# A third pair of k-tiles by seven products in the gate and up projections of a hybrid decoder block

## The chip, the cores and the metric

One Trainium2 chip, and one core of it. The metric is the device time of one execution of the whole program in microseconds. The weights and the activations lie in HBM in float32.

## The reference

One decoder block over 256 tokens of width 2048: a mix of attention heads and mLSTM heads, then a feed-forward layer of width 5632, then a gated per-layer embedding. The change lies in the feed-forward layer:

```python
h2 = rms_norm(x, w_norm_ffn[i])
x = x + (jax.nn.silu(h2 @ w_ffn_gate[i]) * (h2 @ w_ffn_up[i])) @ w_ffn_down[i]
```

`w_ffn_gate` and `w_ffn_up` are 2048 x 5632, `w_ffn_down` is 5632 x 2048. The results are wanted in float32 accuracy.

## The kernel before

TensorE multiplies operands of a shortened float32 type, so each float32 operand is held as two halves: `h`, the value rounded to that type, and `l`, what is left. `halves` (L215) makes the two from a weight piece of 1024 elements per partition: ScalarE casts `wr` to `wh` (L220), and VectorE subtracts to get `wl` (L221). Each product of two float32 tiles is then three matmuls, high by high, high by low and low by high.

Gate and up run over 11 chunks of 512 columns (L769), numbered 1 to 11 here (the program's `c` is one less). A chunk needs the products of 16 k-tiles of 128 rows with two blocks of 128 tokens and two weights. The k-tiles are taken in eight pairs, 0 to 7, and each pair is one *unit*. A **plain unit** (L685) loads 512 KB of gate and 512 KB of up, makes halves of both, and issues 24 matmuls: two k-tiles, two token blocks, two weights, three matmuls each. Its results go to four banks of PSUM, P2, P3, P4 and P8.

Pairs 1 and 2 are **seven units** (L699). A pair of k-tiles, two token blocks and the two weights form a 2 x 2 by 2 x 2 product, which Strassen's scheme in Winograd's form does with seven block products where the plain way has eight. The four combinations of the activations, `fh` and `fl`, are made once for all chunks (`make_forms`, L657). The combinations of the weights are made anew in every chunk: four adds of 512 elements on VectorE (L702, L703, L705, L706) into two tiles `wt`, and then halves of the gate piece, of both `wt` tiles and of half the up piece. So a seven unit issues 21 matmuls and makes four `wh` and `wl` tiles, where a plain unit issues 24 and makes two. Its products P1, P6, P7 and P5 have banks of their own. After the last seven unit of a chunk these are drained (L748 to L755: a ScalarE copy and four VectorE adds), and at the end of the chunk VectorE folds the eight banks and forms silu(gate) times up (L757 to L766, with a sigmoid on ScalarE), then transposes it blockwise (L187). The transposed tile goes to HBM and back through GpSimd's queue (L191, L196), and is split in halves some units later (L129, L130).

All eight banks are in use; the two groups of four change roles from chunk to chunk (L718). The pool for weights (L34) has four buffers each of `wr`, `wh` and `wl`. A load waits in SyncE's queue until the buffer of two units before is free. The engines run in parallel, each strictly in its own order, and wait by semaphores. The order on each engine is set when the program is built, by a scheduler that places what it takes to be ready: neither the source's order nor a change in one line tells where an instruction stands.

Of the kernel before, what the change touches and what calls it, by code (L numbers as in the profile page):

```python
# [7 lines left out]
F32 = mybir.dt.float32  # L8
F32R = mybir.dt.float32r
BF16 = mybir.dt.bfloat16  # L10
# [9 lines left out]
def block_kernel(ctx, tc, x, p, w_norm_mix, w_in, fox_f_bias, q_norm_w, k_norm_w, conv_w, conv_b,  # L20
# [39 lines left out]
    rows_b = const.tile([82, P], F32, name="rows_b")  # L60

# [51 lines left out]
    def sumsq(dst, src):  # L113
        sq = small.tile([P, 512], BF16, name="sq")
        n = src.shape[-1]
        nc.scalar.activation(sq[:, 0:n], src, AF.Square, accum_out=dst)
# [151 lines left out]
    with tc.tile_pool(name="mixp", bufs=1) as mp:  # L268
# [40 lines left out]
        tasks = {}  # L309

# [334 lines left out]
    with tc.tile_pool(name="ffnp", bufs=1) as fp:  # L645
        acts_g = []

        def after_up(dst, gg):
            yield from split_by_blocks(dst, lambda b: gg[b])
# [3 lines left out]
        seven = (1, 2)  # L653
        first_order, later_order = (0, 3, 4, 1, 5, 2, 6, 7), (0, 3, 1, 4, 5, 2, 6, 7)
# [44 lines left out]
        def seven_unit(c, p):  # L699
            ra, rb = (load_piece(w, 2 * p, 2, c * 512, 512) for w in (w_gate, w_up))  # L700
            t12 = fp.tile([P, 2, 512], F32, name="wt", bufs=2)
            nc.vector.tensor_tensor(t12[:, 0], ra[:, 0], rb[:, 0], op=ALU.subtract)  # L702
            nc.vector.tensor_tensor(t12[:, 1], t12[:, 0], rb[:, 1], op=ALU.add)  # L703
            t34 = fp.tile([P, 2, 512], F32, name="wt", bufs=2)
            nc.vector.tensor_tensor(t34[:, 0], t12[:, 1], ra[:, 0], op=ALU.subtract)  # L705
            nc.vector.tensor_tensor(t34[:, 1], ra[:, 1], t12[:, 1], op=ALU.subtract)  # L706
            ah, al = halves(ra)
            h12, l12 = halves(t12)
            bh, bl = halves(rb[:, 1:2])
            h34, l34 = halves(t34)  # L710
            right = {"P1": (ah[:, 0], al[:, 0]), "P6": (h12[:, 1], l12[:, 1]), "P5": (h12[:, 0], l12[:, 0]),
                     "P2": (ah[:, 1], al[:, 1]), "P7": (h34[:, 0], l34[:, 0]), "P4": (h34[:, 1], l34[:, 1]),
# [3 lines left out]
        def gate_up(c):  # L716
# [4 lines left out]
            order = first_order if c == 0 else later_order  # L721
            left = {"P1": len(seven), "P6": len(seven), "P7": len(seven), "P5": len(seven), "P8": 16 - 2 * len(seven),
                    **{n: 16 - len(seven) for n in ("P2", "P3", "P4")}}
            bank, t1, qr, su = {}, None, None, None
            for p in order:
                advance(1)
                if p in seven:
# [8 lines left out]
                advance(1)  # L736
                for n, (lh, ll), (rh, rl) in unit:
# [7 lines left out]
                if su is None and left["P1"] == 0:  # L745
                    while held:
                        advance(1)
                    t1 = fp.tile([P, 512], F32, name="sg", bufs=2)  # L748
                    nc.scalar.copy(t1, bank["P1"])
                    qr = quads.tile([P, 2, 512], F32, name="quad")  # L750
# [112 lines left out]
```

## Time and profile before

| | |
|---|---|
| median of 3 runs | 1221.85 us (1220.7 to 1222.06) |
| the profiled execution | 1227.3 us |
| its span, first to last instruction | 1225.1 us |
| busy: TensorE, VectorE, ScalarE | 1211.5, 854.3, 622.8 us |
| granted TensorE clock, mean | 0.998 |
| gate and up, from the end of chunk 1 to the end of chunk 11 | 431.5 us |

A busy time is the time in which an engine had an instruction under way. TensorE's matmuls overlap: one takes 0.39 us from start to end, and the next starts after 0.23 us. So a group's mean duration is not what a matmul costs; the step from start to start is. The same holds, by less, for VectorE, whose instructions overlap by some 0.08 us. The time of a stage is read from the start of an instruction that occurs once per chunk.

### The profile page before, as it was taken

To read this page: it belongs to the slowest core of one execution; us is meant where nothing else is said; L and a number is where in the kernel's file an instruction comes from. 1 tells how busy PE (TensorE), PEld (TensorE's weight loads), DVE (VectorE), ACT (ScalarE), POOL (GpSimd) and SP (SyncE) were. 2 spreads that over 40 slices of the span, in tenths; PEclk is the share of its full clock that TensorE was granted. 3 is DMA by queue.
4 is the path that set the end of the run, shared out by engine and by line. 5 is a ranking of instruction groups with operands and counts; after the bars stand their busy time and mean duration, and the time that the engine had idled before them with its cause. 6 is when DMAs were issued, how large, how long until landed. Compare 5 with 4: busy or idle time off the path is not lost. (4 is left out here: it accounts for less than half of the span.)

```text
span 1225.1 us, 15485 instructions
## 1 busy us (share of the span) xinstructions
PE 1211.5 (99%) x5609; PEld 1003.9 (82%) x5609; DVE 854.3 (70%) x1188; ACT 622.8 (51%) x823; POOL 79.5 (6%) x149
## 2 busy tenths in 40 slices
PE   9999999999999999999999999999999999999998
PEld 6899978878888787888788888878888888888888
DVE  5766755565565898888879889888855554545754
ACT  6555556545555545555544555554544444446542
POOL 1111000000011000000000000000000000000000
PEclk9999999999999999999999999999999999999999
DMA  7677744575678667676676776667676666665762
GB/s 262 213 233 221 236 138 131 173 227 157 202 239 254 192 204 232 219 217 210 209 253 194 234 219 216 222 208 251 201 262 206 212 210 210 208 206 170 232 227 92
DMA packets 136384, 257.33 MB, mean 210 GB/s; under 512 B 10002, under 2 KB 29300, under 8 KB 136308
## 3 DMA queue, kind: packets, MB, share of 16 engines
q1 hardware_dynamic: 127156, 229.06, 59.2%
q0 software_dynamic: 8400, 26.22, 6.6%
q8 instruction: 44, 0.72, 0.2%
q10 hardware_dynamic: 752, 1.06, 0.2%
q14 instruction: 32, 0.26, 0.1%
HBM read 241.10 MB, written 15.20 MB: 209 GB/s over the span
## 5 line engine op out<-in xcount | busy, mean ns | idle before, releaser
L221 DVE TENSOR_TENSOR wl<-wr,wh 128x1024 fp32r<-128x1024 f32 (+2 forms) x445 | 508.6, 1154 | 289.4 <-ACT wh L220 288.5
L220 ACT CAST wh<-wr 128x1024 fp32r<-128x1024 f32 (+2 forms) x445 | 439.0, 997 | 449.2 <-PE acc L264 259.1
L262 PE MATMUL acc<-wh,act_h 128*128 128x512 f32 (+2 forms) x864 | 320.6, 371 | 0.1
L263 PE MATMUL acc<-wl,act_h 128*128 128x512 f32 (+2 forms) x864 | 318.0, 368 | 1.6 <-DVE wl L221 1.6
L264 PE MATMUL acc<-wh,act_l 128*128 128x512 f32 (+2 forms) x864 | 317.8, 368 | 0.0
L263 PEld LDWEIGHTS acc<-wl,act_h 128*128 128x128 f32 x864 | 163.0, 189 | 25.8 <-DVE wl L221 2.9
L262 PEld LDWEIGHTS acc<-wh,act_h 128*128 128x128 f32 x864 | 163.1, 189 | 24.6 <-ACT act_h L133 0.9
L264 PEld LDWEIGHTS acc<-wh,act_l 128*128 128x128 f32 x864 | 162.8, 188 | 24.5 <-DVE act_l L135 0.6
L191 POOL DMA_DIRECT2D swap<-tq x100 | 61.0, 616 | 882.1 <-DVE tq L187 882.1
L743 PE MATMUL acc<-wl,act_h 128*128 128x512 f32 x272 | 107.0, 393 | 0.1
L744 PE MATMUL acc<-wh,act_l 128*128 128x512 f32 x272 | 106.0, 390 | 0.0
L742 PE MATMUL acc<-wh,act_h 128*128 128x512 f32 x272 | 103.7, 390 | 0.0
L263 PE MATMUL acc<-wl,gh 128*128 128x512 f32 x224 | 88.3, 394 | 0.0
L262 PE MATMUL acc<-wh,gh 128*128 128x512 f32 x224 | 87.8, 392 | 0.0
L264 PE MATMUL acc<-wh,gl 128*128 128x512 f32 x224 | 86.9, 388 | 0.0
L220 ACT CAST wh<-wt 128x1024 fp32r<-128x1024 f32 x44 | 46.2, 1050 | 55.4 <-DVE wt L703 54.4
L742 PE MATMUL tr<-wh,act_h 128*128 128x512 f32 x178 | 69.5, 391 | 0.2 <-ACT wh L220 0.2
L743 PE MATMUL tr<-wl,act_h 128*128 128x512 f32 x178 | 69.7, 392 | 0.0
L744 PE MATMUL tr<-wh,act_l 128*128 128x512 f32 x178 | 69.3, 389 | 0.0
L743 PEld LDWEIGHTS acc<-wl,act_h 128*128 128x128 f32 x272 | 51.0, 188 | 13.7 <-DVE wl L221 3.3
L742 PEld LDWEIGHTS acc<-wh,act_h 128*128 128x128 f32 x272 | 51.1, 188 | 11.0
L744 PEld LDWEIGHTS acc<-wh,act_l 128*128 128x128 f32 x272 | 51.1, 188 | 10.4
(259 smaller groups left out, 1328.2 us busy)
## 6 DMA issues: line engine op xcount, KB each, us to landing
wr<-in_w_ffn_gate_dram SPq DMA_DIRECT2D x88, 512.0 KB, 3.5
wr<-in_w_ffn_up_dram SPq DMA_DIRECT2D x88, 512.0 KB, 4.5
wr<-in_w_ffn_down_dram SPq DMA_DIRECT2D x88, 512.0 KB, 4.6
wr<-in_w_in_dram SPq DMA_DIRECT2D x63, 512.0 KB, 4.7
wr<-in_w_in_dram SPq DMA_DIRECT2D x48, 344.0 KB, 3.7
wr<-in_w_out_dram SPq DMA_DIRECT2D x32, 512.0 KB, 4.3
wr<-in_w_ple_gate_dram SPq DMA_DIRECT2D x32, 512.0 KB, 4.6
swap<-tq POOLq DMA_DIRECT2D x100, 128.0 KB, 3.6
```

Source lines behind the costliest of these rows:

```text
L191: nc.gpsimd.dma_start(out=d[:, :, :, i, :].rearrange("j c b e -> c b j e"), in_=t[32 * i:32 * i + 32].rearrange("c b j k r -> c b j (k r)"))
L220: nc.scalar.copy(wh, wr)
L221: nc.vector.tensor_tensor(wl, wr, wh.bitcast(F32), op=ALU.subtract)
L262: nc.tensor.matmul(po[b][:, 0:n], ah[:, kk, s], wh[:, j, :], start=count == 1, stop=False)
L263: nc.tensor.matmul(po[b][:, 0:n], ah[:, kk, s], wl[:, j, :], start=False, stop=False)
L264: nc.tensor.matmul(po[b][:, 0:n], al[:, kk, s], wh[:, j, :], start=False, stop=count == total)
L742: nc.tensor.matmul(bank[n], lh, rh, start=first, stop=False)
L743: nc.tensor.matmul(bank[n], lh, rl, start=False, stop=False)
L744: nc.tensor.matmul(bank[n], ll, rh, start=False, stop=left[n] == 0)
```

## The change

From chunk 2 on, pair 4 is a seven unit too, and the order of the units becomes 0, 3, 1, 5, 2, 6, 4, 7. Chunk 1 keeps two seven units. The forms of pair 4 are made once, in chunk 2. Inside a seven unit the halves of the gate piece come first, then the first `wt` and its halves, then the second and its halves, and at the end those of the up piece; the products go P1, P2, P6, P5, P7, P4, P3. The draining of P1, P6, P7 and P5 stands one unit later in the source, behind the loads and halves of the unit that follows. The sigmoids write into the tile `quad` that the drained sums leave. To make room, `rows_b` moves to a pool that ends before gate and up, `sq` has one buffer in place of two, `t1` has a tile of its own, and at the end `acts_p` and the weights of the last norm use the two `wt` tiles (two loads of 1024 columns where there were four of 512). The way through HBM waits three units in place of two at each step.

```diff
-        seven = (1, 2)
-        first_order, later_order = (0, 3, 4, 1, 5, 2, 6, 7), (0, 3, 1, 4, 5, 2, 6, 7)
+        first_seven, seven = (1, 2), (1, 2, 4)
+        first_order, later_order = (0, 3, 4, 1, 5, 2, 6, 7), (0, 3, 1, 5, 2, 6, 4, 7)
...
             ra, rb = (load_piece(w, 2 * p, 2, c * 512, 512) for w in (w_gate, w_up))
+            ah, al = halves(ra)
             t12 = fp.tile([P, 2, 512], F32, name="wt", bufs=2)
             nc.vector.tensor_tensor(t12[:, 0], ra[:, 0], rb[:, 0], op=ALU.subtract)
             nc.vector.tensor_tensor(t12[:, 1], t12[:, 0], rb[:, 1], op=ALU.add)
+            h12, l12 = halves(t12)
             t34 = fp.tile([P, 2, 512], F32, name="wt", bufs=2)
             nc.vector.tensor_tensor(t34[:, 0], t12[:, 1], ra[:, 0], op=ALU.subtract)
             nc.vector.tensor_tensor(t34[:, 1], ra[:, 1], t12[:, 1], op=ALU.subtract)
-            ah, al = halves(ra)
-            h12, l12 = halves(t12)
+            h34, l34 = halves(t34)
             bh, bl = halves(rb[:, 1:2])
-            h34, l34 = halves(t34)
-            right = {"P1": (ah[:, 0], al[:, 0]), "P6": (h12[:, 1], l12[:, 1]), "P5": (h12[:, 0], l12[:, 0]),
-                     "P2": (ah[:, 1], al[:, 1]), "P7": (h34[:, 0], l34[:, 0]), "P4": (h34[:, 1], l34[:, 1]),
+            right = {"P1": (ah[:, 0], al[:, 0]), "P2": (ah[:, 1], al[:, 1]), "P6": (h12[:, 1], l12[:, 1]),
+                     "P5": (h12[:, 0], l12[:, 0]), "P7": (h34[:, 0], l34[:, 0]), "P4": (h34[:, 1], l34[:, 1]),
                      "P3": (bh[:, 0], bl[:, 0])}
...
-                if p in seven:
+                if p in by_seven:
...
+                if su is None and left["P1"] == 0:
+                    while held:
+                        advance(1)
+                    t1 = fp.tile([P, 512], F32, name="t1")
+                    nc.scalar.copy(t1, bank["P1"])
...
                 for n, (lh, ll), (rh, rl) in unit:
...
-                if su is None and left["P1"] == 0:
-                    while held:
-                        advance(1)
-                    t1 = fp.tile([P, 512], F32, name="sg", bufs=2)
-                    nc.scalar.copy(t1, bank["P1"])
...
-                sg = fp.tile([P, 512], F32, name="sg", bufs=2)
+                sg = qr[:, b]
...
-            if c == 0:
-                for kp in seven:
-                    Task(make_forms(kp), [made_by[id(acts_h[kp // 2][0])]])
+            for kp in (first_seven, [kp for kp in seven if kp not in first_seven], ())[min(c, 2)]:
+                Task(make_forms(kp), [made_by[id(acts_h[kp // 2][0])]])
```

The change moves instructions on every engine of this stage. In what follows `wl` and `wh` are halves of weights with their buffer numbers; line numbers of the changed file are up to two less in the first part and shift by a few in the second.

VectorE at the end of chunk 4, before. `wl_5213` is the up half of pair 0 of chunk 5, and `wl_5252` and `wl_5258` are the halves of its pair 3:

```order
L221 TENSOR_TENSOR wl_5213<-wr_5210,wh_5212 128x1024
L757 TENSOR_TENSOR gg0_5185<-acc0_4865,sg_5105 128x512
L759 TENSOR_TENSOR tq_5110<-acc1_4869,tq_5110 128x512
L758 TENSOR_TENSOR gg1_5186<-acc0_4873,quad_5107 128x512
L765 SCALAR_TENSOR_TENSOR gg0_5185<-gg0_5185,rstd_ffn_3032,sg_5191 128x512
L760 TENSOR_TENSOR tq_5110<-acc1_4877,tq_5110 128x512
L766 SCALAR_TENSOR_TENSOR gg0_5185<-tq_5110,rstd_ffn_3032,gg0_5185 128x512
L765 SCALAR_TENSOR_TENSOR gg1_5186<-gg1_5186,rstd_ffn_3032,sg_5195 128x512
L221 TENSOR_TENSOR wl_5252<-wr_5249,wh_5251 128x1024
L766 SCALAR_TENSOR_TENSOR gg1_5186<-tq_5110,rstd_ffn_3032,gg1_5186 128x512
L221 TENSOR_TENSOR wl_5258<-wr_5255,wh_5257 128x1024
L187 STREAM_TRANSPOSE tq_5201<-gg0_5185 128x512
```

and now, where `wl_5243` and `wl_5249` are the gate and the up half of pair 0 of chunk 5:

```order
L219 TENSOR_TENSOR wl_5243<-wr_5240,wh_5242 128x1024
L756 TENSOR_TENSOR gg0_5223<-acc0_4892,t1_5191 128x512
L758 TENSOR_TENSOR tq_5196<-acc1_4896,tq_5196 128x512
L757 TENSOR_TENSOR gg1_5224<-acc0_4900,quad_5193 128x512
L759 TENSOR_TENSOR tq_5196<-acc1_4904,tq_5196 128x512
L764 SCALAR_TENSOR_TENSOR gg0_5223<-gg0_5223,rstd_ffn_3032,quad_5193 128x512
L764 SCALAR_TENSOR_TENSOR gg1_5224<-gg1_5224,rstd_ffn_3032,quad_5193 128x512
L765 SCALAR_TENSOR_TENSOR gg0_5223<-tq_5196,rstd_ffn_3032,gg0_5223 128x512
L765 SCALAR_TENSOR_TENSOR gg1_5224<-tq_5196,rstd_ffn_3032,gg1_5224 128x512
L219 TENSOR_TENSOR wl_5249<-wr_5246,wh_5248 128x1024
L185 STREAM_TRANSPOSE tq_5237<-gg0_5223 128x512
```

The up half of chunk 5's first unit stood ahead of the fold of chunk 4 and now stands behind all of it, behind the instruction that waits for chunk 4's last product (L760, now L759). Chunks 2, 4, 6, 8 and 10 end like this; chunks 3, 5, 7 and 9 have that half inside the fold, behind its first instruction, and the transposes between the two halves of pair 3.

TensorE some 14 matmuls into chunk 5, now (`wh_5242` is of pair 0's gate, `wh_5287` of pair 3's, `wh_5327` of pair 1's gate):

```order
L752 MATMUL tr_5265<-wh_5242,act_h_3209 128x512
L753 MATMUL tr_5265<-wl_5243,act_h_3209 128x512
L754 MATMUL tr_5265<-wh_5242,act_l_3210 128x512
L752 MATMUL tr_5257<-wh_5287,act_h_3381 128x512
L752 MATMUL tr_5265<-wh_5287,act_h_3381 128x512
L752 MATMUL acc0_5349<-wh_5327,act_h_3209 128x512
L753 MATMUL sc_5261<-wl_5249,act_h_3209 128x512
L754 MATMUL sc_5261<-wh_5248,act_l_3210 128x512
L753 MATMUL sc_5269<-wl_5249,act_h_3209 128x512
L754 MATMUL sc_5269<-wh_5248,act_l_3210 128x512
```

Before, the first matmul with pair 0's low up half was the fifth of a chunk. Now (`wl_5249`) it is the 18th, behind matmuls of pairs 3 and 1 that need only high halves.

VectorE in chunk 5 from pair 5's gate half (`wl_5377`) to pair 2's, now (`wr_5414` and `wr_5416` are pair 2's gate and up loads, `wt_5422` its first sums, `wl_5426` their low half):

```order
L219 TENSOR_TENSOR wl_5377<-wr_5374,wh_5376 128x1024
L219 TENSOR_TENSOR wl_5383<-wr_5380,wh_5382 128x1024
L219 TENSOR_TENSOR wl_5419<-wr_5414,wh_5418 128x1024
L702 TENSOR_TENSOR wt_5422<-wr_5414,wr_5416 128x512
L128 TENSOR_TENSOR act_l_5236<-quad_5321,act_h_5235 128x512 x2
L703 TENSOR_TENSOR wt_5422<-wt_5422,wr_5416 128x512
L706 TENSOR_TENSOR wt_5429<-wt_5422,wr_5414 128x512
L707 TENSOR_TENSOR wt_5429<-wr_5414,wt_5422 128x512
L219 TENSOR_TENSOR wl_5426<-wt_5422,wh_5425 128x1024
```

Before, the halves that come back from HBM (L130, now L128) stood ahead of L702. They now stand between L702 and L703 of pair 2, which moved from the sixth to the fifth place of the chunk.

## Rows read from the trace of the kernel before

**Rows 1.** The page, busy time of each engine over the span.

```profile
PE 1211.5 (99%) x5609; PEld 1003.9 (82%) x5609; DVE 854.3 (70%) x1188; ACT 622.8 (51%) x823; POOL 79.5 (6%) x149
```

**Rows 2.** Windows view, gate and up: busy us (count) by engine, clock, DMA share.

```profile
447.00:877.00 430.00, 428.24 (x1856) 345.09 (x1855) 370.02 (x440) 225.30 (x250) 29.91 (x50) 1.00 0.69 219
```

**Rows 3.** View of line L757, once per chunk: first and last start.

```profile
L757 DVE TENSOR_TENSOR gg<-tr,sg x6: 681/684/692, 446.6 to 878.1; 128x512 f32<-128x512 f32 x6
```

**Rows 4.** Timeline of TensorE: a plain unit, a seven unit, a wait.

```profile
500.52 0.39 PE L742 MATMUL tr<-wh,act_h 128*128 128x512 f32 x1
...
502.33 0.39 PE L744 MATMUL acc<-wh,act_l 128*128 128x512 f32 x1
...
503.44 0.40 PE L744 MATMUL acc<-wh,fl 128*128 128x512 f32 x1
...
507.16 0.40 PE L742 MATMUL tr<-wh,act_h 128*128 128x512 f32 x1
...
606.11 0.50 PE L743 MATMUL acc<-wl,fh 128*128 128x512 f32 x1 [0.26 <-DVE wl L221]
606.45 0.39 PE L744 MATMUL acc<-wh,fl 128*128 128x512 f32 x1
```

**Rows 5.** Timeline of VectorE at the end of chunk 2: start, us.

```profile
492.11 0.68 DVE L760 TENSOR_TENSOR tq<-acc,tq 128x512 f32<-128x512 f32 x1
492.71 0.74 DVE L766 SCALAR_TENSOR_TENSOR gg<-tq,rstd_ffn,gg 128x512 f32<-128x512 f32 x1
493.37 0.74 DVE L765 SCALAR_TENSOR_TENSOR gg<-gg,rstd_ffn,sg 128x512 f32<-128x512 f32 x1
494.04 1.22 DVE L221 TENSOR_TENSOR wl<-wr,wh 128x1024 fp32r<-128x1024 f32 x1
495.17 0.74 DVE L766 SCALAR_TENSOR_TENSOR gg<-tq,rstd_ffn,gg 128x512 f32<-128x512 f32 x1
...
496.97 1.29 DVE L187 STREAM_TRANSPOSE tq<-gg 128x512 f32<-128x512 f32 x2
498.19 0.65 DVE L702 TENSOR_TENSOR wt<-wr 128x512 f32<-128x512 f32 x1
```

**Rows 6.** Timeline of VectorE in a seven unit of chunk 5.

```profile
599.96 1.29 DVE L130 TENSOR_TENSOR act_l<-quad,act_h 128x512 fp32r<-128x512 f32 x2
601.17 0.69 DVE L702 TENSOR_TENSOR wt<-wr 128x512 f32<-128x512 f32 x1
601.89 0.69 DVE L703 TENSOR_TENSOR wt<-wt,wr 128x512 f32<-128x512 f32 x1
...
604.84 1.22 DVE L221 TENSOR_TENSOR wl<-wt,wh 128x1024 fp32r<-128x1024 f32 x1
605.97 0.68 DVE L221 TENSOR_TENSOR wl<-wr,wh 128x512 fp32r<-128x512 f32 x1
606.58 1.22 DVE L221 TENSOR_TENSOR wl<-wt,wh 128x1024 fp32r<-128x1024 f32 x1
```

**Rows 7.** Timeline of ScalarE: a cast that waited for a load.

```profile
553.70 1.05 ACT L220 CAST wh<-wr 128x1024 fp32r<-128x1024 f32 x1 [3.27 <-DMA wr<-in_w_ffn_up_dram]
```

**Rows 8.** Waits of VectorE in gate and up: us, times, longest.

```profile
DVE wl L221 <- ACT wh L220: 51.7, 49, 3.5
```

**Rows 9.** DMA view: three single loads, from issue to landing in us.

```profile
wr<-in_w_ffn_gate_dram SPq DMA_DIRECT2D x1, 512.0 KB, 3.4
wr<-in_w_ffn_up_dram SPq DMA_DIRECT2D x1, 512.0 KB, 4.4
wr<-in_w_ffn_up_dram SPq DMA_DIRECT2D x1, 512.0 KB, 7.2
```

**Rows 10.** Timeline of GpSimd's queue in chunk 4: the way through HBM.

```profile
541.39 2.44 POOL L191 DMA_DIRECT2D swap<-tq  x4 [36.48 <-DVE tq L187]
546.88 0.56 POOL L196 DMA_DIRECT2D quad<-swap  x1 [3.05 <-DMA swap<-tq]
```

**Rows 11.** Lines view, VectorE: one of a form's four small sums.

```profile
L675 DVE TENSOR_TENSOR quad<-tq,quad 128x128 f32<-128x128 f32 x2 | 0.6, 283 | 0.0
```

More of the change, by code (lines that the diff above doesn't have):

```diff
@@ L58, in load_x @@
         nc.sync.dma_start(out=xres[:, :, c0:c1], in_=x_v[:, :, c0:c1])
-    rows_b = const.tile([82, P], F32, name="rows_b")
     def load_rows_b():
@@ L113, in sumsq @@
     def sumsq(dst, src):
-        sq = small.tile([P, 512], BF16, name="sq")
+        sq = small.tile([P, 512], BF16, name="sq", bufs=1)
         n = src.shape[-1]
@@ L309, in block_kernel @@
         tasks = {}
+        rows_b = mp.tile([82, P], F32, name="rows_b")
         def params():
@@ L648, in after_up @@
         def after_up(dst, gg):
-            yield from split_by_blocks(dst, lambda b: gg[b])
-        seven = (1, 2)
-        first_order, later_order = (0, 3, 4, 1, 5, 2, 6, 7), (0, 3, 1, 4, 5, 2, 6, 7)
+            yield from split_by_blocks(dst, lambda b: gg[b], gap=3)
+        first_seven, seven = (1, 2), (1, 2, 4)
+        first_order, later_order = (0, 3, 4, 1, 5, 2, 6, 7), (0, 3, 1, 5, 2, 6, 4, 7)
         forms = {}
@@ L720, in gate_up @@
                     "P2": shared[0], "P3": shared[1], "P4": shared[0], "P8": shared[1]}
-            order = first_order if c == 0 else later_order
-            left = {"P1": len(seven), "P6": len(seven), "P7": len(seven), "P5": len(seven), "P8": 16 - 2 * len(seven),
-                    **{n: 16 - len(seven) for n in ("P2", "P3", "P4")}}
+            order, by_seven = (later_order, seven) if c else (first_order, first_seven)
+            n7 = len(by_seven)
+            left = {**{n: n7 for n in ("P1", "P6", "P7", "P5")}, **{n: 16 - n7 for n in ("P2", "P3", "P4")}, "P8": 16 - 2 * n7}
             bank, t1, qr, su = {}, None, None, None
@@ L736, in gate_up @@
                 advance(1)
+                if su is None and left["P1"] == 0:
[3 more added lines that the diff above has]
+                    nc.scalar.copy(t1, bank["P1"])
+                    qr = quads.tile([P, 2, 512], F32, name="quad")
+                    nc.vector.tensor_tensor(qr[:, 0], bank["P6"], t1, op=ALU.add)
+                    nc.vector.tensor_tensor(qr[:, 1], bank["P7"], qr[:, 0], op=ALU.add)
+                    su = quads.tile([P, 2, 512], F32, name="tq")
+                    for i in range(2):
+                        nc.vector.tensor_tensor(su[:, i], bank["P5"], qr[:, i], op=ALU.add)
                 for n, (lh, ll), (rh, rl) in unit:
@@ L778, in block_kernel @@
             made_by[id(acts_g[c][0])] = Task(after_up(acts_g[c], gg))
-        acts_p = [fp.tile([P, 2, 256], F32R, name="wt", bufs=2) for _ in range(2)]
+        acts_p = fp.tile([P, 2, 2, 256], F32R, name="wt", bufs=2)
+        acts_p = [acts_p[:, i] for i in range(2)]
         def load_p():
```

15 lines of the change are left out of this document (5 added, 10 removed).

## The prediction

> **What bounds the kernel now.** Read the busy times first: TensorE is busy for 99% of the span, VectorE for 70% [rows 1]. That is an average over stages, so next comes the window of gate and up, where the change lies: there VectorE is busy for 370.0 of 430 us, 86%, ScalarE for 52%, and TensorE's clock is granted in full [rows 2]. Line L757 runs once per chunk; from the end of chunk 1 to that of chunk 11 its starts are 431.5 us apart, 43.15 us a chunk [rows 3]. TensorE's timeline gives the steps. In a plain unit eight matmuls take 502.33 - 500.52 us, 0.227 each, so a unit of 24 takes 5.44. In a seven unit sixteen steps take 3.72 us, 0.2325 each, so 21 take 4.88 [rows 4]. A chunk of six plain and two seven units would take 42.40; it takes 43.15. The missing 0.75 us are short waits, and the same group shows one: a matmul with a low half starts at 606.11, where VectorE's subtraction of that half ran from 604.84 for 1.22 us [rows 4, 6]. The matmul behind it comes after 0.34 us, not 0.23, so a wait costs 0.11 more than itself. VectorE is already late for some units. TensorE is the bound with VectorE just behind it.
>
> **What goes.** Ten chunks turn a plain unit into a seven unit: 5.44 - 4.88 = 0.56 us each. The ideal chunk becomes 5 x 5.44 + 3 x 4.88 = 41.84.
>
> **What comes on VectorE.** From start to start, a subtraction of 1024 elements takes 1.13 us, one of 512 takes 0.60, a fused multiply 0.66, a transpose 0.61 [rows 5], and an add that needs the one before it 0.72 [rows 6]. A plain unit is two subtractions, 2.26. A seven unit is four adds, three long subtractions and a short one, 2.64 + 3.39 + 0.60 = 6.6. So VectorE gets 4.4 us more per chunk: its busy 37.1 us (86% of 43.15) become 41.5, in a chunk that would take 41.84. Almost every wait of VectorE now becomes one of TensorE. In these ten chunks it waits 51.7 us for casts alone [rows 8]. Most of that is VectorE ahead of the buffers, which vanishes when it is late. What remains I follow through a chunk; t is the time from the chunk's first matmul.
>
> **Chunks 3, 5, 7, 9 and 11: the start.** The up half of the first unit stands behind the fold. The last product of the chunk before is there at t = 0.25 (its matmul starts at -0.23 and takes 0.39, and a hand-over takes 0.1). Then come one add, four fused multiplies and the half itself: 0.25 + 0.60 + 4 x 0.66 = 3.49, and at 3.49 + 1.22 = 4.71 it is done. TensorE's 18th matmul needs it; its turn would be at 17 x 0.227 = 3.85. With 0.05 for the hand-over it waits 0.9 us. The cast of pair 1's gate, which the 17th needs, frees at the same time: its buffer is read until 3.35, and a cast takes 1.05 [rows 7]. Beside the work before it the added wait has no cover.
>
> **Every chunk: pair 2.** Behind the fold VectorE runs to the end of pair 1 at t = 15.0, which frees the up buffer that pair 2's up load waits for. Loads land 3.4 us after issue alone, 4.4 behind another, 7.2 beside the way through HBM [rows 9]. In the chunk shown that way reads back 5.5 us after its first write is issued [rows 10], about t = 12 here, so the load at 15.1 meets its tail. I take 4.3, the middle case: t = 19.4. Behind it on VectorE stand the first add, 0.60, the two returned halves, 1.21 [rows 6], which now stand inside this chain, three adds, 0.72 + 0.72 + 0.60, and the subtraction, 1.22: the half is there at 24.5. TensorE needs it at the eighth matmul of pair 2. Two plain units, pair 1, one plain unit and the first wait make that 0.93 + 3 x 5.44 + 4.88 + 7 x 0.2325 = 23.76. A wait of 0.75. In chunks 4, 6, 8 and 10, which do not begin with the wait above, TensorE is there 0.8 us sooner, and VectorE, whose fold is spread otherwise, 0.3 sooner: 1.15, and 0.16 for pair 1's second sums. Pair 4 follows 10.3 us later by the same loop (load, sums, halves), which takes 0.1 + 4.0 + 5.9 us: level with TensorE, no further wait. After it the draining (0.60) and the halves of pair 7 are due by a margin of 0.2 to 0.4; I add nothing.
>
> **The sum.** Each wait costs 0.11 more, and about 0.2 a chunk remains of the small gaps that are there today. Five chunks at 41.84 + 0.93 + 0.75 + 0.22 + 0.20 = 43.94 and four at 41.84 + 0.16 + 1.15 + 0.22 + 0.20 = 43.57. Chunk 2 starts without the wait, but makes the forms of pair 4: four sums of 0.28 [rows 11] and two operations of 512, some 2.3 us of VectorE, of which I put 1.75 on the path: 43.9. Together 219.7 + 174.3 + 43.9 = 437.9 for 431.5: **6.4 us slower**. The profiled execution took 1227.3 (span 1225.1, and 2.2 around it), so 1233.7; it lies 5.4 above the median of 1221.85, which becomes **1228.3 us**.
>
> The ends: loads at 3.4 us take 0.3 off a chunk of the first kind (VectorE itself is then late) and 0.5 off one of the second, 1.5 + 2.0, so 1225. At 5.3 us, half way between 3.4 and 7.2, they add 1.0 in nine chunks: 1237.
>
> Against the rows stands a rule of the Trainium skill, "DMA: Bandwidth & Descriptors", section "Anatomy of one DMA — SWDGE (gpsimd) path": a transfer costs about 2.0 us and its bytes at 436 GB/s. By it 512 KB would land in 3.2 us, an estimate, and the sum would be 1225 or less. The trace has 3.4 for a load alone and more for two, and the pair's two loads do overlap, so the rows decide.
>
> **What I cost at nothing.** `rows_b`, `sq` and `acts_p` only change places; their work lies in other stages, on the same engines and in the same number of operations. The third step on the way through HBM makes the returned halves later, but nothing needs them before the down projection. The two wider loads of the last norm are as many bytes. ScalarE gets 1.5 casts of 1.05 us more per chunk and stays below 60%.
>
> **Rivals.**
> - *VectorE keeps up (faster).* The chain of pair 2 gets its load early or VectorE gains on an earlier unit; new orders of products (P6 two places later) give it 0.7 us more than today in each seven unit. Then only the wait at the start remains, and it decides: 5 x 43.08 + 4 x 42.1 + 42.3 = 426.1, 5.4 us less than now, 1216.5. It turns where pair 2's up load lands by t = 18.4. For it: the waits today are mostly in pairs whose low half is due at the fifth matmul. Against it: 41.5 of 41.84.
> - *The full gain.* No wait at all, 418.4: 1208.8. Against it stands the order at the chunk's start, which no load can mend.
> - *Loads collide (slower still).* Pair 2's loads meet the read from HBM and take 7.2 us as in rows 9: 2.9 more per chunk. In every second of nine chunks 13 more, 1241; in all 1254. For it: the read is issued at t = 12, as pair 2's gate load is.
> - *No effect.* That the change doesn't do what it says is excluded by the order: 30 matmuls fewer. But the waits may take up the gain and no more.
>
> **How the numbers follow.** Two runs of this kernel can be told apart from 0.2%, 2.4 us. The forecast 0.55, of which 0.10 within 2.4 us. VectorE keeps up 0.22, of which 0.03 within. Full gain 0.04. Collisions 0.15. No effect 0.04. So faster 0.23, the same 0.17, slower 0.60. The range runs from 1215, which holds most of the second case, to 1241, which holds the collisions in half the chunks; the forecast's own is 1225 to 1237.
>
> **What would show it.** Right: L756 (today L757) some 43.7 us apart, VectorE busy over 95% in gate and up, TensorE waiting for L219 near the 18th matmul of every odd chunk and in pair 2, hardly in pairs 1 and 4. Wrong: chunks below 43 us, VectorE's waits for casts unchanged, or TensorE waiting for a load or a cast in place of a subtraction.

## The result and the profile after

The changed kernel takes 1252.62 us (median of 4 runs, 1247.59 to 1253.87), the kernel before 1221.95 (4 runs). The ratio is 1.0233, 95% interval 1.0215 to 1.0252: slower, as forecast, but by 30.7 us where the prediction had 6.4, and above its range. The profiled execution took 1253.87 us, its span is 1252.2. (Of run e12 below only the median of ten executions is told; the eleventh, the profiled one, was disturbed: 1711 us, with the clock at 0.75 throughout.)

The whole loss lies where the change was made. On the page of the changed kernel, TensorE is busy as long as before [rows 1] in a span that is 27 us longer; in the windows view of gate and up VectorE is busy 415 of 460 us, 90%, and the clock is no longer granted in full [rows 2]:

```profile
PE 1214.5 (97%) x5579; PEld 1002.2 (80%) x5579; DVE 902.8 (72%) x1254; ACT 640.2 (51%) x844; POOL 79.8 (6%) x149
```

```profile
447.00:907.00 460.00, 433.08 (x1823) 344.70 (x1822) 415.42 (x504) 239.62 (x270) 30.01 (x50) 0.98 0.64 205
```

The line that runs once per chunk, now L756:

```profile
L756 DVE TENSOR_TENSOR gg<-tr,t x6: 690/692/692, 441.4 to 903.4; 128x512 f32<-128x512 f32 x6
```

Ten chunks take 903.4 - 441.4 = 462.0 us, before 431.5 [rows 3]: 30.5 more. (The profiled execution of before is 5.4 us above its median; its stage begins at 446.6, 5.2 us later than here, so that excess lies ahead of the stage for the most part.) Between the starts of L756 in turn lie 44.5, 44.2, 45.4, 47.8, 46.5, 44.5, 48.2, 48.1, 44.4 and 48.4 us. So there are two kinds of chunk: five of 44.2 to 45.4, 0.3 to 1.8 us above the prediction's 43.6 to 43.9, and five long ones, 5, 6, 8, 9 and 11, of 46.5 to 48.4.

The waits of the stage, by engine (us in all, times, longest):

```profile
PE acc L752 <- ACT wh L218: 12.0, 10, 2.8
PE tr L753 <- DVE wl L219: 4.9, 5, 1.3
PE acc L753 <- DVE wl L219: 4.3, 6, 0.8
PE tr L752 <- ACT wh L218: 2.8, 2, 1.5
...
DVE wt L702 <- DMA wr<-in_w_ffn_up_dram: 24.1, 14, 3.7
DVE wl L219 <- ACT wh L218: 14.3, 21, 1.2
...
ACT gh L127 <- DMA quad<-swap: 21.7, 6, 4.3
...
ACT act_h L127 <- DMA quad<-swap: 9.7, 4, 3.9
```

The same waits for up loads and for the read in the kernel before:

```profile
DVE wt L702 <- DMA wr<-in_w_ffn_up_dram: 6.2, 5, 2.4
...
ACT gh L129 <- DMA quad<-swap: 0.6, 2, 0.4
```

VectorE's wait for casts shrank, from 51.7 [rows 8]; what has grown is its wait for up loads, to 24 us, and ScalarE's for the read from HBM, to 31 us. Nearly all of both falls in pair 2. TensorE in turn waits for the casts of its weights (`wh`) more than for their subtractions (`wl`). The timeline of a long chunk, the fifth, from the issue of pair 2's loads to its first matmuls (start, duration, engine; the idle time and its releaser in brackets):

```profile
589.32 0.37 SPq L210 DMA_DIRECT2D wr<-in_w_ffn_gate_dram  x1
592.30 0.37 SPq L210 DMA_DIRECT2D wr<-in_w_ffn_up_dram  x1
593.44 0.47 SPq L210 DMA_DIRECT2D wr<-in_w_ffn_gate_dram  x1
594.57 0.60 SPq L210 DMA_DIRECT2D wr<-in_w_ffn_up_dram  x1
...
591.69 0.57 POOL L194 DMA_DIRECT2D quad<-swap  x1 [5.62 <-DMA swap<-tq]
...
598.78 1.14 ACT L127 CAST act_h<-quad 128x512 fp32r<-128x512 f32 x2 [3.94 <-DMA quad<-swap]
...
599.50 0.69 DVE L702 TENSOR_TENSOR wt<-wr 128x512 f32<-128x512 f32 x1 [3.40 <-DMA wr<-in_w_ffn_up_dram]
600.11 1.28 DVE L128 TENSOR_TENSOR act_l<-quad,act_h 128x512 fp32r<-128x512 f32 x2
...
600.60 0.39 PE L754 MATMUL tr<-wh,act_l 128*128 128x512 f32 x1
603.21 0.50 PE L752 MATMUL acc<-wh,fh 128*128 128x512 f32 x1 [2.22 <-ACT wh L218]
604.51 0.50 PE L753 MATMUL acc<-wl,fh 128*128 128x512 f32 x1 [0.81 <-DVE wl L219]
...
605.47 0.63 PE L753 MATMUL acc<-wl,fh 128*128 128x512 f32 x1
605.90 0.63 PE L754 MATMUL acc<-wh,fl 128*128 128x512 f32 x1
606.33 0.63 PE L752 MATMUL acc<-wh,fh 128*128 128x512 f32 x1
```

Pair 2's up load is issued at 592.30 and lands at 599.50, 7.2 us later. Within little more than five microseconds are issued the gate load ahead of it, the read of 512 KB from HBM 0.6 us ahead of it, the load itself, and two loads behind it. The read lands for ScalarE at 598.78, so the returned halves (L127, L128) arrive at the same late moment in the same chain. TensorE stands from 601.0 to 603.2, and again before the low half. Behind that its steps are 0.43 us where they were 0.23. The windows view of the same stretch shows what the transfers reached and what the clock did:

```profile
595.00:599.00 4.00, 4.00 (x19) 3.32 (x18) 1.10 (x1) 0.22 (x1) 0.00 (x0) 1.00 0.90 316
599.00:603.00 4.00, 1.99 (x9) 1.31 (x7) 3.46 (x6) 1.81 (x3) 0.00 (x0) 1.00 0.17 64
603.00:605.00 2.00, 0.99 (x3) 0.62 (x4) 1.95 (x3) 1.72 (x4) 0.00 (x0) 1.00 0.22 33
605.00:608.00 3.00, 3.00 (x9) 2.31 (x8) 2.83 (x4) 2.00 (x3) 0.00 (x0) 0.52 0.59 180
```

While the load is late the DMA engines are 90% busy and move 316 GB/s, in a stage that needs 205 on average: the transfers share them. Then, with all buffers full, they move 33 to 64. What makes one chunk long and the next not is less clear. In chunk 7 the same five transfers are issued, the read 0.2 us ahead of the load instead of 0.6, and the load is there after 5.4 us; in chunk 10 it takes 4.1. In the five long chunks it takes 6.9 to 7.8. No run was made to find out what decides. TensorE was busy for half of 599 to 605, and then has 0.52 of its clock for 3 us: the 1.2 GHz level. In four of the five long chunks such a stretch follows; 34 steps of some 0.43 us lie in them, 6.6 us more than at 0.2325 each.

The collision itself is not new. In the kernel before, the way through HBM reads at the same place of every chunk, right behind the up load of pair 5, a plain unit (chunk 5, SyncE's and GpSimd's queues and ScalarE):

```profile
589.85 0.37 SPq L212 DMA_DIRECT2D wr<-in_w_ffn_up_dram  x1
590.27 0.56 POOL L196 DMA_DIRECT2D quad<-swap  x1 [2.98 <-DMA swap<-tq]
...
597.74 1.05 ACT L220 CAST wh<-wr 128x1024 fp32r<-128x1024 f32 x1 [3.85 <-DMA wr<-in_w_ffn_up_dram]
```

There too the load lands late, 4.6 to 7.8 us after its issue in the ten chunks, 7.8 in the one shown, and yet no wait of TensorE is longer than 0.26 us in these chunks. What the change did was to put a seven unit, with a longer chain behind its up load, and a nearly full VectorE at this place.

### The profile page after: what moved, and what is told of

It is laid out like the page before. It is cut to its first block, busy times and chain, and to the rows that moved or that the text cites. A ratio compares the mean times of both kernels' runs of the same rounds, so it can differ in the third digit from the quotient of the medians.

```text
span 1252.2 us, 15535 instructions
## 1 busy us (share of the span) xinstructions
PE 1214.5 (97%) x5579; PEld 1002.2 (80%) x5579; DVE 902.8 (72%) x1254; ACT 640.2 (51%) x844; POOL 79.8 (6%) x149
## 4 chain that ended last, share of the span: by engine, by line
PE 63%; DVE 17%; DMA 12%; issue 4%; ACT 3%; POOL 1%; SPq 0%; ACTq 0%; DVEq 0%; POOLq 0%
PE acc L261 15%; PE acc L260 15%; PE acc L262 15%; DVE wl L219 7%; DMA wr<-in_w_ffn_up_dram 5%; PE acc L753 3%; PE acc L754 3%; DMA quad<-swap 3%; PE acc L752 2%; ACT wh L218 2%; DMA wr<-in_w_in_dram 2%; DMA swap<-tq 2%; PE sc L753 1%; PE tr L753 1%; PE tr L754 1%
## 5 line engine op out<-in xcount | busy, mean ns | idle before, releaser
L219 DVE TENSOR_TENSOR wl<-wr,wh 128x1024 fp32r<-128x1024 f32 (+2 forms) x445 | 500.6, 1141 | 240.5 <-ACT wh L218 239.6
L218 ACT CAST wh<-wr 128x1024 fp32r<-128x1024 f32 (+2 forms) x445 | 434.6, 986 | 360.1 <-PE acc L262 260.7
L260 PEld LDWEIGHTS acc<-wh,act_h 128*128 128x128 f32 x864 | 162.7, 188 | 24.8 <-ACT act_h L131 1.4
L261 PEld LDWEIGHTS acc<-wl,act_h 128*128 128x128 f32 x864 | 162.7, 188 | 24.2 <-DVE wl L219 1.5
L262 PEld LDWEIGHTS acc<-wh,act_l 128*128 128x128 f32 x864 | 162.5, 188 | 24.4 <-DVE act_l L133 0.6
L218 ACT CAST wh<-wt 128x1024 fp32r<-128x1024 f32 x64 | 67.1, 1049 | 124.3 <-DVE wt L703 86.9
L752 PE MATMUL acc<-wh,act_h 128*128 128x512 f32 x247 | 94.3, 393 | 3.6 <-ACT wh L218 3.6
L753 PE MATMUL acc<-wl,act_h 128*128 128x512 f32 x247 | 96.2, 392 | 0.4 <-DVE wl L219 0.3
L754 PE MATMUL acc<-wh,act_l 128*128 128x512 f32 x247 | 95.9, 391 | 0.0
L219 DVE TENSOR_TENSOR wl<-wt,wh 128x1024 fp32r<-128x1024 f32 x64 | 78.2, 1222 | 8.8 <-ACT wh L218 7.4
L752 PEld LDWEIGHTS acc<-wh,act_h 128*128 128x128 f32 x247 | 46.7, 189 | 15.4 <-ACT wh L218 5.7
L753 PEld LDWEIGHTS acc<-wl,act_h 128*128 128x128 f32 x247 | 46.5, 188 | 12.1 <-DVE wl L219 2.2
```

The lines of the kernel that those rows point to most:

```text
L218: nc.scalar.copy(wh, wr)
L219: nc.vector.tensor_tensor(wl, wr, wh.bitcast(F32), op=ALU.subtract)
L260: nc.tensor.matmul(po[b][:, 0:n], ah[:, kk, s], wh[:, j, :], start=count == 1, stop=False)
L261: nc.tensor.matmul(po[b][:, 0:n], ah[:, kk, s], wl[:, j, :], start=False, stop=False)
L262: nc.tensor.matmul(po[b][:, 0:n], al[:, kk, s], wh[:, j, :], start=False, stop=count == total)
L752: nc.tensor.matmul(bank[n], lh, rh, start=first, stop=False)
```

## The experiments

Theory A: pair 2's up load and the read from HBM share the bandwidth, and what waits for both stands in one chain. Theory B: VectorE's work, 41.5 us in a chunk of 41.84, is the loss by itself. Theory C: the new orders are. "Stage" is from the first to the last start of the line that was L756. In the expectations from the fifth on, t counts from that line's start (575.49 in chunk 5), 1.8 us ahead of the chunk's first matmul, where the prediction's t begins.

| run | edit to the changed kernel | median us | ratio to before, 95% | stage us |
|---|---|---|---|---|
| before | | 1221.95 | | 431.5 |
| changed | | 1252.62 | 1.0233 (1.0215 to 1.0252) | 462.0 |
| e1 | two seven units | 1232.28 | 1.0065 (1.0045 to 1.0086) | 436.2 |
| e2 | no way through HBM | 1231.39 | 1.0054 (1.0033 to 1.0074) | 439.1 |
| e3 | up half second | 1240.12 | 1.0120 (1.0094 to 1.0147) | 445.3 |
| e4 | gap 4 | 1255.68 | 1.0250 (1.0223 to 1.0278) | 463.4 |
| e5 | way through HBM later | 1230.92 | 1.0065 (1.0039 to 1.0090) | 437.3 |
| e6 | up half second, silu | 1223.61 | 1.0012 (0.9995 to 1.0029) | 433.9 |
| e7 | e6 and e5 | 1220.47 | 0.9976 (0.9962 to 0.9991) | 425.5 |
| e8 | e6 with two seven units | 1219.86 | 0.9972 (0.9960 to 0.9983) | 425.5 |
| e9 | silu | 1233.09 | 1.0080 (1.0053 to 1.0107) | 444.7 |
| e10 | e5 and silu | 1228.87 | 1.0045 (1.0029 to 1.0061) | 436.5 |
| e11 | the kernel before, with silu | 1219.92 | 0.9970 (0.9956 to 0.9984) | 428.8 |
| e12 | e7, one sum on GpSimd | 1225.40 | 1.0008 (0.9992 to 1.0025) | |
| e13 | the read left out | 1231.06 | 1.0070 (1.0046 to 1.0093) | 438.0 |
| e14 | read later (did not move) | 1254.93 | 1.0263 (1.0234 to 1.0292) | 459.4 |
| e15 | read held behind pair 2's load | 1249.61 | 1.0213 (1.0186 to 1.0241) | 452.7 |

**e1, two seven units in the new order.**

```diff
-        first_seven, seven = (1, 2), (1, 2, 4)
+        first_seven, seven = (1, 2), (1, 2)
```

> Chunks 2 to 11 take pairs 1 and 2 by seven products and pair 4 as a plain unit; everything else stays as in the changed kernel (order of units, of halves and of products, third step on the way through HBM). VectorE has 4.4 us less per chunk than in the changed kernel, TensorE 0.56 more. Theory A (pair 2's up load lands late, because it shares the bandwidth with its neighbours and with the way through HBM, and the returned halves stand in the same chain): pair 2's chain has the same load and the same returned halves ahead of it, so most of the 30 us stays: 1240 to 1255. Theory B (VectorE's capacity: 41.5 us of work in a chunk of 41.84): VectorE falls back to 37 us per chunk and the loss goes: 1215 to 1226. Theory C (the new orders cost by themselves, whatever the third pair): 1250 or more, with the waits spread over pairs 1 and 2.

It lies between the theories: the stage loses 4.7 us to before, not 25 and not none. Pair 2's up load still comes late (13.8 us of VectorE's waits, ten times), but by 0.2 to 3.2 us, and VectorE, with 4.4 us less to do, makes about half of it good (TensorE waits 7.5 us in all); TensorE's waits there are 0.1 to 0.8, once 1.3. (The loads are also shorter here, 4.0 to 5.7 us in nine of ten chunks.) Theory C falls as the main cause, and A alone does not do: that a late load costs so much fits a VectorE with nothing in hand.

**e2 and e13, the way through HBM left out, and its read alone.**

```diff
+        if gap == 3:
+            for _ in range(2 * gap):
+                yield
+            return t.rearrange("p b j k r -> p (b j k r)")...
         for _ in range(gap):
             yield
         q = quads.tile([P, 8, 4, 32], F32, name="quad")
```

(In e2 the lines stand ahead of the writes, in e13, as shown, behind them. The way is 512 KB each way per chunk; the expectation's 256 KB is a slip.)

> The activation of gate and up is not sent through HBM: its halves are cut from the tile that VectorE has transposed within blocks of 32, so the output is not the reference's (the rest of the transposition is left out: four writes and one read of 256 KB in all each way per chunk). All of VectorE's and ScalarE's operations stay, at the same places in their order. Theory A: the loads of pair 2 have the bandwidth to themselves and land in 3.4 to 4.6 us, the returned halves no longer wait, TensorE's waits in pair 2 fall below 1 us and its clock stays up: 1218 to 1230. Theory B: VectorE has as much to do as before, 1248 or more. Theory C: 1248 or more.

> The changed kernel with the four writes of the way through HBM kept and the read left out: the returned halves are cut from the tile that VectorE has transposed within blocks, so the output is not the reference's (the read of 512 KB per chunk and the transposition that it completes are left out). If the read is what pair 2's up load meets (it is issued at t = 15.7 to 16.8, the load at 16.6 to 16.8): as without the way through HBM, 1229 to 1236. If the writes (t = 8 to 16) already push the loads together: 1243 or more. VectorE and ScalarE have the same operations as in the changed kernel.

Both take 1231 us (for e2 just above the range of A), and both stages are 438 to 439 us. Where they stand here, the writes cost nothing; without the read 462.0 - 438.0 = 24 us go. VectorE has the same work as in the changed kernel (414.5 us busy), so B alone cannot account for those 24. But its order is not the same, though the expectations said so: the halves no longer wait for a read, and the scheduler has moved them from pair 2 to pair 1, in chunk 5 of e13 to t = 11.4, where it was 24.6 in the changed kernel:

```profile
585.56 0.68 DVE L128 TENSOR_TENSOR act_l<-tq,act_h 128x512 fp32r<-128x512 f32 x1
```

So these runs take the late load and the late halves out of pair 2 together. In e13, the view of L760 (which was L756), the window of gate and up, and VectorE's waits:

```profile
L760 DVE TENSOR_TENSOR gg<-tr,t x6: 684/692/692, 441.6 to 879.6; 128x512 f32<-128x512 f32 x6
```

```profile
447.00:885.00 438.00, 425.83 (x1829) 339.96 (x1829) 414.53 (x505) 241.52 (x272) 24.29 (x40) 1.00 0.66 204
```

```profile
DVE wl L223 <- ACT wh L222: 12.9, 13, 1.2
DVE wt L706 <- DMA wr<-in_w_ffn_up_dram: 5.1, 15, 0.5
```

The wait for up loads is 5.1 us in place of 24.1, none over 0.5. The clock is 1.00, and TensorE's busy time is 433.08 - 425.83 = 7.3 us less for the same matmuls: by a second way, about what the clock had cost. VectorE is now at 95%, and nine of ten chunks take 43.7 to 44.2 us: this is what is left for B, 438.0 - 431.5 = 6.5 us. It stands in pair 1, in waits of 0.4, 0.56 and 0.24 us in most chunks, where the halves now are.

**e5, the whole way through HBM later.**

```diff
             yield held
+        for _ in range(6 if gap == 3 else 0):
+            yield
+        while held:
+            yield held
         held.append(srcs)
```

> The whole way through HBM of gate and up (the transposes on VectorE, the four writes, the read and the returned halves) begins six steps later, behind pair 1's work: the writes are issued about t = 19 in place of 9, the read about 25 in place of 16, and the returned halves stand behind pair 4's. Work and bytes are the same. Theory A (pair 2's up load is late because it meets the read): pair 2's load, issued at 16.7, lands in 4 us, VectorE's 24 us of waits for it fall below 8, TensorE's long waits at t = 26 to 29 go, and the stage falls from 462 to 440 to 448, 1230 to 1240; if the later read then meets pair 4's up load (issued at 29 to 32), the waits move to pair 4 and the time stays at 1245 or more. Theory B (VectorE's capacity): no change, 1250 to 1255.

The scheduler moved the read by 2.4 to 3.9 us in chunks 3 to 11 and not by nine, and that was enough. In chunk 5 of e5, the SyncE and GpSimd queues and VectorE:

```profile
591.43 0.37 SPq L214 DMA_DIRECT2D wr<-in_w_ffn_up_dram  x1
...
594.14 0.57 POOL L198 DMA_DIRECT2D quad<-swap  x1 [4.81 <-DMA swap<-tq]
...
596.12 0.69 DVE L706 TENSOR_TENSOR wt<-wr 128x512 f32<-128x512 f32 x1
...
601.80 1.29 DVE L128 TENSOR_TENSOR act_l<-quad,act_h 128x512 fp32r<-128x512 f32 x2
```

The read is issued 2.7 us behind the up load, the load is there within 4.7 us, VectorE starts without a wait, and the returned halves stand behind pair 2's sums. The last nine chunks take 43.1 to 44.2 us, the stage 437.3. The bytes, the work and the number of transfers are those of the changed kernel: the place of the way through HBM and of its halves was worth 25 us. Chunk 2 shows that it matters what else stands there: its four writes are issued at t = 14.0 to 15.8, the load at 16.0 lands after 5.8 us, and the chunk takes 45.7.

**e4 and e14, two edits that moved little.**

```diff
-            yield from split_by_blocks(dst, lambda b: gg[b], gap=3)
+            yield from split_by_blocks(dst, lambda b: gg[b], gap=4)
```

```diff
+        if gap == 3:
+            for _ in range(5):
+                yield
+            nc.scalar.copy(quads.tile([P, 8, 4, 32], F32, name="quad")[:, 0, 0, :], ident[:, 0:32])
         q = quads.tile([P, 8, 4, 32], F32, name="quad")
...
-        for _ in range(gap):
+        for _ in range(5 if gap == 3 else gap):
```

> The read from HBM and the returned halves come one step later each (four steps in place of three): the halves stand behind all of pair 2's work on ScalarE and VectorE, not in front of its first sums. Loads and buffers are as before. Theory A: ScalarE's wait for the read (21.7 us in all) and 1.2 us of VectorE's work leave pair 2's chain, only the late load stays: 1232 to 1245. If the load alone sets the end, 1248 to 1255. Theory B: the same work on VectorE, 1250 to 1255.

> The changed kernel with the read alone issued later: the buffer into which it reads is first written by a copy of 32 columns on ScalarE that stands behind pair 2's casts, so the read starts at about t = 27, and the returned halves stand behind pair 4's. The writes stay at t = 8 to 16. If the read is what the load meets: pair 2's up load lands in 4 to 5 us, no chunk is longer than 45 us, 1230 to 1238. If the writes are: 1245 or more. If the read now meets pair 4's loads (issued at 28 to 31): long waits at t = 36 to 38, 1240 or more.

Neither does what was meant. In chunk 5 of e4 a returned half still starts right behind pair 2's first sum (605.78, and 605.17 for the sum). In e14 the copy, which waits for nothing, ran at 585.13 in chunk 5, t = 4.1 where 27 was meant, and from chunk 3 on the reads are issued at t = 15.9 to 17.2, about as in the changed kernel. Both times are about those of the changed kernel: that says how steady the loss is, and nothing on the halves.

**e15, the read held by data until pair 2's load is there.**

```diff
             h12, l12 = halves(t12)
+            last_half[0] = h12
...
+        if gap == 3:
+            for _ in range(5):
+                yield
+            nc.scalar.copy(quads.tile([P, 8, 4, 32], F32, name="quad")[:, 0, 0, :], last_half[0][:, 0, 0:32].bitcast(F32))
         q = quads.tile([P, 8, 4, 32], F32, name="quad")
...
-        for _ in range(gap):
+        for _ in range(5 if gap == 3 else gap):
```

> As the run before meant it, and now tied by data: the copy of 32 columns that the read's buffer waits for takes them from the rounded first sums of pair 2, which are only there once pair 2's up load has landed. So the read cannot start before that, about t = 22. The number that decides is VectorE's wait for pair 2's up load: 24 us in all in the changed kernel. If the read is what the load meets: below 8 us. The time then depends on where the returned halves stand: on ScalarE they come three casts behind the copy, before the up cast of the unit after pair 2, and the read needs 4 to 6 us, so TensorE may wait in that unit in place of pair 2; 1230 to 1245. If the load is late all the same: 20 us of waits and 1250 or more.

Its waits, of TensorE, VectorE and ScalarE:

```profile
PE acc L758 <- ACT wh L223: 8.8, 11, 1.4
PE sc L758 <- ACT wh L223: 5.3, 6, 1.4
...
DVE gl L128 <- ACT gh L127: 9.7, 6, 2.0
...
DVE wt L707 <- DMA wr<-in_w_ffn_up_dram: 2.5, 6, 0.6
...
ACT gh L127 <- DMA quad<-swap: 13.8, 6, 2.8
```

The load is in time (2.5 us in place of 24.1), which shows that the read is what it met. But the time falls by 3 us only, less than expected: ScalarE now waits for the read ahead of the casts of the unit behind pair 2, and TensorE stands there at t = 30 to 32, for 0.6 to 1.4 and 0.76 us in every chunk. So the read can cost in two ways, by the load and by the returned halves, which in pair 2 came due together. With the load in time, 452.7 - 438.0 = 14.7 of the 24 us stay. Not all of that is the halves': chunks 4, 6, 8 and 10 now also begin with a wait of 0.73, which they did not have. The late load alone was not tried, since e4 did not move the halves, so how the 24 us divide is not shown.

**e3, the up half second in a seven unit, and P3 the third product.**

```diff
             ah, al = halves(ra)
+            bh, bl = halves(rb[:, 1:2])
             t12 = fp.tile([P, 2, 512], F32, name="wt", bufs=2)
...
             h34, l34 = halves(t34)
-            bh, bl = halves(rb[:, 1:2])
...
```

> In a seven unit the half of the up piece (used by P3) is cut second, right behind the gate's, and P3 is the third product; the sums and halves of the others follow. The up buffer is then free after the first sums, about 3.5 us sooner, and so is the next load into it issued. Theory A: pair 2's up load is issued at t = 11.5 in place of 15.1 and lands 2.5 to 3.5 us sooner, unless the read from HBM, issued at about 14, then binds: 1228 to 1243. Theory B: VectorE does the same work, 1250 to 1255.

As A has it: in most chunks the load is issued some 2 us sooner, and nine of ten chunks take 42.8 to 44.8 us. VectorE itself waits for no up load any more; ScalarE's cast of the up half, which now comes ahead of VectorE's sums, takes these waits (49.6 us of ScalarE's time, against 9.4 in the changed kernel). What is left for TensorE are 0.73 us at the start of nine chunks and 0.2 to 0.9 in pair 2.

**e9, e6, e10 and e7, less work on VectorE.**

```diff
-                nc.scalar.activation(sg, gg[b], AF.Sigmoid, scale=r)
-                nc.vector.scalar_tensor_tensor(gg[b], gg[b], r, sg, op0=ALU.mult, op1=ALU.mult)
-                nc.vector.scalar_tensor_tensor(gg[b], su[:, b], r, gg[b], op0=ALU.mult, op1=ALU.mult)
+                nc.scalar.activation(sg, gg[b], AF.Silu, scale=r)
+                nc.vector.scalar_tensor_tensor(gg[b], su[:, b], r, sg, op0=ALU.mult, op1=ALU.mult)
```

> The changed kernel with silu in one activation alone: 1.3 us less on VectorE per chunk, nothing else moved. Theory A (the late load sets the long waits): the load of pair 2 and the way through HBM both come 1.3 us sooner and meet as before; VectorE's waits for pair 2's up load stay at 20 us or more in all and so do TensorE's long ones, only the start of the chunk and the tightness behind it gain, 4 to 9 us: 1243 to 1249. Theory B (VectorE's capacity sets the chunk): 13 us or more go, 1239 or less, and the waits for the load shrink with it.

> The up half second, as in the run that gained 12 us, and besides the fold of each chunk takes silu of the scaled gate in one activation on ScalarE in place of a sigmoid there and a fused multiply of 0.66 us on VectorE: 1.3 us less on VectorE per chunk, and as much less between the last matmul of a chunk and the first half of the next. Theory A2 (with the late load out of the way, VectorE's work and the start of the chunk are what is left, 445 us where TensorE alone would need 418): the waits of 0.73 at t = 6 go and each of ten chunks gets 0.8 to 1.3 us shorter, 1227 to 1233. If what is left is still loads that collide: 1237 to 1242.

> Silu in one activation and the way through HBM six steps later, the halves and products in the changed kernel's order. If the late load and VectorE's work are separate terms, this gains what each gained: 1231 less some 10, 1218 to 1224. If the up half must also come second for the loads to be in time, 1226 or more.

> The three edits together: the up half second, silu on ScalarE, and the way through HBM six steps later. Theory A with A2: no load is late and VectorE has 40.2 us per chunk for a chunk of 41.84: 42.0 to 42.8 per chunk, 1211 to 1219. If the way through HBM costs wherever it lies: 1227 or more.

e9 is a miss for A: 1233 where it said 1243 or more. The long chunks did not stay, they fell from five to three (47.7, 46.7, 46.8), and the others to 41.7 to 44.1. So 1.3 us of VectorE's work decide not only the length of a chunk but how often it meets the read badly; the two causes are no separate terms. In e10 VectorE waits for up loads again, 10.4 us in all, so that the later way through HBM needs the up half second to be enough. It is not the read that the load meets there. In chunk 6 of e10 the four writes are issued just ahead of the load, and the read only when VectorE has started on it:

```profile
630.08 2.44 POOL L193 DMA_DIRECT2D swap<-tq  x4 [39.35 <-DVE tq L189]
632.10 0.37 SPq L214 DMA_DIRECT2D wr<-in_w_ffn_up_dram  x1
...
638.15 0.69 DVE L706 TENSOR_TENSOR wt<-wr 128x512 f32<-128x512 f32 x1 [2.56 <-DMA wr<-in_w_ffn_up_dram]
638.52 0.56 POOL L198 DMA_DIRECT2D quad<-swap  x1 [6.00 <-DMA swap<-tq]
```

So in e10, as in chunk 2 of e5, the late load has the writes beside it and not the read. e6 came out 3 us better than was said, e7 just above its range. In e7 and e8, the window of gate and up:

```profile
441.00:872.00 431.00, 429.33 (x1857) 345.20 (x1856) 406.30 (x492) 238.87 (x276) 29.95 (x50) 1.00 0.70 222
```

```profile
444.00:877.00 433.00, 433.00 (x1895) 353.74 (x1894) 365.94 (x430) 227.44 (x256) 29.98 (x50) 1.00 0.70 222
```

**e8 and e11, two seven units with silu.** The edits are those above, in e11 to the kernel before, in its own order.

> Two seven units per chunk (pairs 1 and 2, as before the change) in the changed kernel's order of units, with the up half second and silu on ScalarE. TensorE alone would need 42.40 per chunk, VectorE has 35.8. If the 0.47 us per chunk that two seven units lost in the new order were the late load of pair 2 (waits of 0.4 to 0.8 at t = 25 to 28), they go and the chunk takes 42.4 to 42.9: 1214 to 1220. If the new order of units costs by itself, 1225 to 1232.

> The kernel before, with silu in one activation and nothing else. There VectorE is busy for 86% of gate and up and TensorE waits little: at most the small waits go (42.40 in place of 43.15 per chunk), 1214 to 1222. If it gains as much as the version with two seven units in the new order (3.6 us less than before), that gain is silu's and not the order's.

In e8 TensorE is never without a matmul under way (433.00 of 433.00), and its ten chunks take 425.5 us, 42.55 each. e7, with a third seven unit and 30 matmuls fewer in these chunks, takes 425.5 as well: with the late loads gone its VectorE is still at 94%, and the saving of 10 x 0.56 us does not appear. The traces show where it goes: 58 of TensorE's steps from start to start take 0.30 us or more in e7 and 28 in e8; over 0.23 us each they cost 8.4 and 2.9 us, and the 5.5 us between them are the saving. What each of them waited for was not followed further. The version that beats both kernels is one of these three, 0.24 to 0.30% faster than before with intervals that overlap; e11 is the smallest edit, and has no third seven unit.

**e12, one sum of each seven unit on GpSimd.**

```diff
-            nc.vector.tensor_tensor(t34[:, 1], ra[:, 1], t12[:, 1], op=ALU.subtract)
+            nc.gpsimd.tensor_tensor(t34[:, 1], ra[:, 1], t12[:, 1], op=ALU.subtract)
```

> The version with all three edits, and in each seven unit the last of the four sums (for P4) on GpSimd in place of VectorE: 0.6 us less on VectorE three times per chunk. An estimate for GpSimd: 0.44 us for its 128x128 add in the kernel before, four times as many elements, 1.8 us. If VectorE's 94% is what keeps the third seven unit from paying and the engines run beside each other: 41.9 to 42.3 per chunk, 1213 to 1218. If VectorE stands still while GpSimd reads, or the sum comes too late for P4: 1220 to 1235.

By their ratios to before, some 4 us slower than e7 (the intervals do not overlap). Whether VectorE was held up or the sum was late was not settled.

## Why the prediction was wrong

- **What goes, and VectorE's work: right.** 0.56 us per chunk (the page has 5579 matmuls for 5609) and 41.5 us of VectorE per chunk; the profile has 415.4 us in 460, 41.7 per chunk of 46.2.
- **The start of chunks 3, 5, 7, 9 and 11: right in the place.** TensorE's wait for the cast of pair 1's gate is there in all five, 0.73 us; that for pair 0's low up half shows behind it only in chunk 3. TensorE's timeline at the start of chunk 3:

```profile
491.75 0.49 PE L752 MATMUL acc<-wh,act_h 128*128 128x512 f32 x1 [0.73 <-ACT wh L218]
492.48 0.50 PE L753 MATMUL sc<-wl,act_h 128*128 128x512 f32 x1 [0.23 <-DVE wl L219]
```

  Together 0.96 us; forecast was 0.93 for each of the five.
- **Pair 2: this step failed, in its size.** "the load at 15.1 meets its tail. I take 4.3, the middle case". The load was issued at 592.30, 15.0 us behind the first matmul, but the read, put at t = 12, was issued at 14.4 (591.69), since the four writes, begun at 583.63, needed until then: 8 us where 5.5 was taken. So the load met not the read's tail but its beginning, in a burst of five transfers, and is there 4.1 to 7.8 us after issue, 6.1 on average where 4.3 was taken. The trace of before could have shown it: the ten up loads that stood beside the read there took 4.6 to 7.8 us, all above 4.3. The chain in which the wait stands was right; it reaches TensorE at the low half, as said, but at the cast before it too: 2.2 and 0.8 us in the chunk shown where 0.75 was said.
- **The rival "loads collide" is what happened.** It had the mechanism and the price, 2.9 more per chunk, and for all nine chunks 1254; it was given 0.15. Five chunks show it in full: they lie 2.9 to 4.6 us above the sum's, 20.0 in all, of which the clock has 6.6; the other five lie 0.3 to 1.8 above, 4.1 in all. The weight was wrong: the argument for it, that the read is issued when pair 2's loads are, was in the text. That its 1254 lies so near 1252.62 is luck, since five chunks collided in full and not nine, and the clock, which it did not have, made up for part of the rest.
- **What was in no step.** The clock, 6.6 to 7.3 us; and that the returned halves wait for the same read on ScalarE, 31 us, ahead of pair 2's casts. They were counted as 1.21 us of VectorE and their lateness at nothing, because nothing needs them before the down projection; but what stands behind them on ScalarE waits too, 3.94 us in the chunk shown.
- **Without the read the sum holds.** e13's stage is 438.0 and e5's 437.3, the sum was 437.9, but by chance for the most part: in e13 the waits stand in pair 1, not in pair 2, and only chunk 3 begins with one. As to the signs: "hardly in pairs 1 and 4" came true; VectorE over 95% did not (90%, in e13 94.6%), nor did 43.7 us from chunk to chunk. And one of the signs of being wrong came true: TensorE waits for casts, 16 us in all, more than for subtractions, 10 us.
- **The rule.** The Trainium skill, "DMA: Bandwidth & Descriptors", section "Anatomy of one DMA — SWDGE (gpsimd) path", gives about 2.0 us and the bytes at 436 GB/s for a transfer that GpSimd issues; by it 512 KB take 3.2 us, an estimate. The loads, to which the prediction applied it, are issued by SyncE, so it does not speak of them. The read is GpSimd's: 4.2 to 7.5 us from issue to landing in the changed kernel, 3.4 at best (e1), so the trace comes near it for the fastest and disagrees for the rest, which share the DMA engines with the loads.

The account of the 30.5 us, the read taken out first: the read's place, with the late load and the late halves, 24.0, of which the clock has some 7; what is left for VectorE's work, 6.5 (e13 against before). It depends on that order: with 1.3 us per chunk of VectorE's work taken out first, 17.3 go (e9), with 4.4 us and the third seven unit 25.8 (e1). The loss needs both.

## What to carry to other kernels

A step that is moved up by one place moves its loads too: look up what every other queue, the way through HBM above all, has under way at the new moment, and price the load by the transfers issued within a few microseconds of it, not by a middle value. In the changed kernel, whose VectorE is busy for 95% of the stage once the read is out (e13), loads for which it waited 0.7 to 3.7 us became waits of TensorE of 1.0 to 3.6 us; with VectorE at 86%, waits of 0.2 to 2.0 us became 0 to 1.3 in e1 (once 3.2 us became 2.1), and in the kernel before waits of up to 2.4 us became at most 0.2. So unload that engine first (here one activation in place of a sigmoid and a multiply), and only then cut work on the other; in e7 even that brought nothing over e8. And after an edit of the source, see in the trace whether the instruction moved at all.

## What the runs showed of the hardware that was not expected

After two waits that left TensorE busy for half of six microseconds the granted clock fell to 0.52 for some 3 us, in another chunk to 0.50 for 6 (742 to 748): from 2.4 GHz to the 1.2 GHz level. Shorter waits that came more often, 0.4 and 0.56 us in most chunks of e13, left it at 1.00. So two waits of some 3 us together cost 1.4 to 2.5 us again behind themselves. Their sum alone does not tell: 1.33 and 1.29 us in chunk 6 of the changed kernel left the clock at 1.00, 1.32 and 0.81 in chunk 2 of e1 were followed by 0.50 for 3.4 us.
